# Attention scores issued further apart, and two splits moved behind the Gram masking, in a hybrid RWKV-7 and attention layer

## The chip, the cores and the metric

The kernel runs on one core of a Trainium2 chip. Its engines work at the same time, each through a list of its own in a fixed order: TensorE (PE in the profile; PEld are its weight loads), VectorE (DVE), ScalarE (ACT), GpSimd (POOL), and SyncE (SP), which here only issues DMAs. An instruction waits for semaphores that others raise, and everything behind it on its engine waits with it. The metric is the device time of one execution in microseconds; smaller is better.

## What is computed

One decoder layer for 256 tokens of width 1024, in float32. Two token mixers work on the same normalised input, and one combined projection `w_in` feeds both: RWKV-7 with eight heads of 64, a recurrence over time, and a softmax attention with eight heads, which for 256 tokens is one causal block. A gated feed-forward part with a short convolution follows. What bears on the change, cut from the reference:

```python
def step(state, inp):                       # RWKV-7, one token
    r_t, w_t, k_t, v_t, a_t, b_t = inp
    sa = jnp.einsum('bhvk,bhk->bhv', state, a_t)
    state = (state * w_t[:, :, None, :] + sa[..., None] * b_t[:, :, None, :]
             + v_t[..., None] * k_t[:, :, None, :])
    return state, jnp.einsum('bhvk,bhk->bhv', state, r_t)
...
bonus = (jnp.sum(rh * kh * r_k.astype(f32), axis=-1, keepdims=True) * vh).reshape(B, S, C)
g = jax.nn.sigmoid(xg) @ w_gate_up
return ((y + bonus) * g.astype(f32)).astype(z.dtype)
...
s_own = jnp.einsum('bhqd,bhkd->bhqk', q_c, k_own, preferred_element_type=f32) * scale
s_own = jnp.where(causal, s_own, -jnp.inf)
p = jax.nn.softmax(s_all, axis=-1).astype(v.dtype)
...
u_a = y_a @ w_branch_a[l]
u_b = y_b @ w_branch_b[l]
x = x + (g_a * u_a + g_b * u_b) @ w_out[l]
```

## The kernel before

**Matmuls in two halves.** A float32 operand is split in a high part (a cast to fp32r) and a low part (the rest), and three products are added: high by high, high by low, low by high. Every weight tile of 128x1024 goes through `load_next` (a DMA on SP into `raw`, four buffers), `split_hi` (L259, a cast on ACT, `whi`), `split_lo` (L269, a subtraction on DVE, `wlo`, three buffers), and is used by `wst` (L302, L304, L307) or `xst` (L323, L324, L327). Twelve of these matmuls are called a block here; two blocks use up a tile. A new load is issued when a split has freed its buffer, so weights run ahead of PE by a few tiles.

**Threads.** The projection, the recurrence and the attention are generators: `bulk`, `chain`, `att`, and `gn` for the group norm. Each yields two numbers, what it has just put on PE and how long it must now wait for others. A loop (from L1114) keeps a clock of its own and always resumes the first thread in its list that is due; so these numbers set the order in which instructions are written out. Behind that, the framework's scheduler orders each engine by its own estimate of times. On the chip the order is fixed.

**The recurrence in chunks of 64 tokens.** `chain` builds the decayed inputs AR and KB, then the Gram blocks: 64 matmuls in two groups (L668, `pgr`), each group of four PSUM banks multiplied by the mask `gmask` into G (L672, four operations of 128x512 a group). G's diagonal 16x16 blocks go out and back through DRAM by DMAs (L679, L681, into Tb), are inverted on DVE in fifteen dependent steps (L689, L691, ended by a copy, L692), and are scattered by 24 small DMAs into X (L694, L701; sixteen of the last on SP, eight on POOL). Meanwhile PE transposes v (L720, `pv`) and computes Z0 (L732, `pz`). From X the inverse of the 64x64 blocks is made by `below` (L750, `pp`), `masked` (P, L755), `plain` and `turned_` (L767 and L775, `px`) and additions to X (L760). Then come four chunks: L888 and L893, L896, L900, copies to VU (L903 on ACT, L904 on DVE), L910 (`pS`) and L922; the group norm of each chunk follows (L850 to L873) with a transposition on PE (L867, `pc`).

**Bonus and small up-projection.** `bp` is r times k times a column (L781, four operations on DVE, in place in zr). It is split into bph (L784, ACT) and bpl (L785, DVE). xg, the input of the small up-projection `w_gate_up`, is split into xgh (L787, ACT) and xgl (L788, with L791 twice for the short second part, DVE). PE uses them from L803 on. In the source these splits stand behind a wait of 11.5 units that follows Z0.

**Attention.** `att` starts when q, k and v are there. Scores are made in three groups, `parts`: the first 128 queries with all eight heads, then the last 128 with four heads twice. A group is written to two PSUM banks of the tag `at`, which has two in all (L993, `ps`). The diagonal part is masked on its way out by DVE (L996), and for the later queries the other half is copied out by ACT (L999). Then `softmax`: the maximum (L1004, L1005), an exponential for each head on ACT (L1008), the reciprocal (L1010) and the division (L1011). The loop is

```python
            for i, part in enumerate(parts):
                scores(*part)
                yield 0.9, 3.0
                softmax(*part)
```

After it the weights are transposed (L1021) and multiplied with v (L1033).

Of the kernel before, what the change touches and what calls it, by code (L numbers as in the profile page):

```python
# [9 lines left out]
F32 = mybir.dt.float32  # L10
F32R = mybir.dt.float32r
I32 = mybir.dt.int32
AF = mybir.ActivationFunctionType
OP = mybir.AluOpType
# [4 lines left out]
S = 256  # L19
# [18 lines left out]
def body(tc, x, positions, norm1_g, w_in, rwkv_mu, w_decay_up, decay_bias, w_aaa_up,  # L38
# [3 lines left out]
    act, dve, pool, pe = nc.scalar, nc.vector, nc.gpsimd, nc.tensor  # L42
    ctx = ExitStack()
    with ctx:
# [9 lines left out]
        def b8(name, shape):  # L54
            return sb.tile(shape, F32, name=name, tag="b8", bufs=5)

        def b4(name, shape=(128, 4, 256), dt=F32):
            return sb.tile(list(shape), dt, name=name, tag="b4", bufs=NB4)

        def by(name, shape=(128, 4, 256), dt=F32):  # L60

            return cst.tile(list(shape), dt, name=name, tag="by", bufs=4)

        def t1(name, shape=(128, 256), dt=F32):
            return sb.tile(list(shape), dt, name=name, tag="c1", bufs=8)

        def b2(name, shape, dt=F32):
            return sb.tile(shape, dt, name=name, tag="b2", bufs=9)
# [4 lines left out]
        def chp(name="ch"):  # L73
            return ps.tile([128, 512], F32, name=name, tag="ch", bufs=3)
# [41 lines left out]
        gmask = cst.tile([128, 128], F32, name="gmask")  # L116
# [35 lines left out]
        G1, MU, DB, AB, KK_, KA, RK, LG, LB, G2 = 0, 8, 23, 27, 31, 35, 39, 43, 47, 51  # L152
# [10 lines left out]
        def col(i):  # L163
            return par[:, i:i + 1]
# [337 lines left out]
        xg = b2("xg", [128, 2, S])  # L502
# [7 lines left out]
        def flat(t):  # L510
            return t.rearrange("p a b -> p (a b)")
# [7 lines left out]
        def bsl(q):  # L519

            return slice(64 * (1 - q), 64 * (1 - q) + 64)
# [12 lines left out]
        def gslot(ct, c=0):  # L534

            return 8 * (ct % 2) + 4 * (ct // 2) + c
# [13 lines left out]
        def chain():  # L550

            sg, av, kp = b4("sg"), b4("av"), b4("kp")
# [48 lines left out]
            for j in range(2):  # L601
                p = chp("prx").rearrange("p (a t c) -> p a t c", a=2, t=2)
                for a in range(2):
                    ct = 2 * j + a
                    for t in range(2):
                        pe.transpose(p[:, a, t], rx[:, t, ct * 128:ct * 128 + 128], ident)
                for a in range(2):
                    ct = 2 * j + a
                    dve.scalar_tensor_tensor(kk[:, ct], zk[:, ct], col(KK_ + ct),
                                             p[:, a].rearrange("p t c -> p (t c)"),  # L610
                                             op0=OP.mult, op1=OP.mult)
# [9 lines left out]
            def kb(q, u):  # L621
                return KB[half(q), 128 * u + 64 * q:128 * u + 64 * q + 128]
# [13 lines left out]
            zr = zs["r"]  # L636
# [5 lines left out]
            G = [b8(f"G{q}", [128, 16, 128]) for q in range(2)]  # L642
# [3 lines left out]
            def banks(nm):  # L646
                return [[(chp if j else atp)(nm) for _ in range(2)] for j in range(2)]
# [14 lines left out]
            for g in range(2):  # L662
                pg = [[p.rearrange("p (u i) -> p u i", u=4) for p in pj] for pj in banks("pgr")]
                for ct in (2 * g, 2 * g + 1):
                    for c in range(4):
                        u = 4 * ct + c
                        for q, hs in PAR:
                            pe.matmul(pg[ct % 2][q][:, c], kb(q, u), AR[hs, u].rearrange("p a i -> p (a i)"),  # L668
                                      start=True, stop=True)
                for ct in (2 * g, 2 * g + 1):  # L670
                    for q in range(2):
                        dve.tensor_tensor(G[q][:, gslot(ct):gslot(ct) + 4], pg[ct % 2][q],  # L672
                                          gmask[:, None, :].to_broadcast([128, 4, 128]), op=OP.mult)
                yield 2.1, (5.0, 0.1)[g]
            for q, hs in PAR:
                for b in range(4):
                    q0 = bsl(q).start + 16 * b
                    r0 = (q * 4 + b) * 16
                    nc.sync.dma_start(d1[r0:r0 + 16].rearrange("u (j i) -> j u i", j=16),  # L679
                                      G[q][q0:q0 + 16, :, 16 * b:16 * b + 16])  # L680
                nc.sync.dma_start(Tb[hs], d1[hs].rearrange("u (j i) -> u j i", j=16))  # L681
# [46 lines left out]
            for c in range(4):  # L728
                for j in range(2):
                    for q, a in QA:  # L730
                        ct = 2 * j + a
# [43 lines left out]
                        pe.matmul(p[bsl(a), i], P[bsl(a), i], X[bsl(a), 1, 8 * q + i], start=True, stop=True)  # L775
                return p

            yield 0, 11.5
            bp = zr
            for ct in range(4):  # L780
                dve.scalar_tensor_tensor(bp[:, ct], zr[:, ct], col(RK + ct), kp[:, ct],  # L781
                                         op0=OP.mult, op1=OP.mult)
            bph, bpl = by("bph", dt=F32R), by("bpl", dt=F32R)
            act.copy(flat(bph), flat(bp))  # L784
            dve.tensor_tensor(flat(bpl), flat(bp), flat(bph).bitcast(F32), op=OP.subtract)  # L785
            xgh, xgl = b2("xgh", [128, 2, S], F32R), t1("xgl", dt=F32R)
            act.copy(xgh, xg)  # L787
            dve.tensor_tensor(xgl, xg[:, 0], xgh[:, 0].bitcast(F32), op=OP.subtract)  # L788
            for r in (32, 96):
                ws = slice(r, r + 32)  # L790
                dve.tensor_tensor(xgh[ws, 1], xg[ws, 1], xgh[ws, 1].bitcast(F32), op=OP.subtract)  # L791
            yield 0, 2.0
            assert taken[0] == GATE_AT, taken[0]
            wgh, wgl = weights()
# [3 lines left out]
            for j in range(2):  # L798
                p, pg = chp(), chp("pg")
                for i in range(2):  # L800
                    ct = 2 * j + i
# [10 lines left out]
                for i in range(2):  # L812
                    ct = 2 * j + i
# [3 lines left out]
                                             op0=OP.add, op1=OP.mult)  # L817
# [61 lines left out]
            for c in range(4):  # L879
# [4 lines left out]
                if St is not None:  # L884
                    for j in range(2):
                        for q, a in QA:
                            ct = 2 * j + a
                            pe.matmul(pz[q][bsl(a), j], AR[half(q), 4 * ct + c, 0], St[half(q), ct],  # L888
                                      start=j == 0, stop=False, skip_group_check=True)
                    for j in range(2):  # L890
                        for q, a in QA:
                            ct = 2 * j + a
# [13 lines left out]
                if c < 3:  # L906
                    pS = chp("pS").rearrange("p (a n) -> p a n", a=8)
                    for h in range(8):
                        ct, q = divmod(h, 2)
# [9 lines left out]
                for j in range(2):  # L919
                    for q, a in QA:  # L920
                        ct = 2 * j + a
# [43 lines left out]
        def attention():  # L965
            qkT = []
            for i in range(2):
                dT = b4(f"qkT{i}")
                for j in range(2):
                    p = atp("pqk").rearrange("p (a t c) -> p a t c", a=2, t=2)  # L970
                    for a in range(2):
                        for t in range(2):
                            ct = 2 * j + a
# [12 lines left out]
            def scores(t, j, nh, sc):  # L986
                nk = 128 * (t + 1)
                ts = slice(t * 128, t * 128 + 128)
                pq = [atp("ps").rearrange("p (h k) -> p h k", k=nk) for q in range(2)]
                for i in range(nh // 2):  # L990

                    for q, hs in PAR:
                        pe.matmul(pq[q][:, i], qT[hs, 2 * j + i, ts], kT[hs, 2 * j + i, 0:nk],  # L993
                                  start=True, stop=True)
                for q in range(2):
                    dve.tensor_tensor(sc[:, q:nh:2, nk - 128:nk], pq[q][:, :, nk - 128:nk],  # L996
                                      cmask[:, None, :].to_broadcast([128, nh // 2, 128]), op=OP.add)
                    if t:
                        act.copy(sc[:, q:nh:2, 0:128], pq[q][:, :, 0:128])  # L999
# [40 lines left out]

            for i, part in enumerate(parts):
                scores(*part)
                yield 0.9, 3.0
                softmax(*part)
            yield 0, 4.0
            ybh = by("ybh", dt=F32R)
# [177 lines left out]
        for j in range(11):  # L1224
# [13 lines left out]
            for m in range(2):  # L1238
# [6 lines left out]
                                         op0=OP.mult, op1=OP.add)  # L1245
                dve.scalar_tensor_tensor(cv[:, 2:S], pm[:, 0:S - 2], cpar[:, n:n + 1], cv[:, 2:S],
                                         op0=OP.mult, op1=OP.add)
# [11 lines left out]
            if len(prev) == 2:  # L1259
# [3 lines left out]
        ws = [weights(), weights()]  # L1263
# [4 lines left out]
                                 op0=OP.mult, op1=OP.add)  # L1268
        for f, is_ in ((0, (0,)), (1, (0,)), (0, (1,)), (2, (0,)), (1, (1,)), (2, (1,)), (3, (0, 1)), (4, (0, 1))):
# [11 lines left out]
            if 1 in is_:  # L1281
                o = b2("o", [128, n])
                dve.scalar_tensor_tensor(o, fs, rs[:, t:t + 1], pre if f == 4 else x_sb[t][:, cs],
                                         op0=OP.mult, op1=OP.add)
# [25 lines left out]
```

## Time and profile before

| | us |
|---|---|
| median of three runs | 414.85 (414.8 to 416.55) |
| profiled execution | 414.23 |
| its span, first to last instruction | 412.5 |
| PE busy in the span | 402.8 |
| DVE busy | 325.8 |
| ACT busy | 232.8 |

The span is what the trace covers; the 1.73 us beside it belong to the start and the end of the execution. A row of the timeline gives start, duration, engine, line, operation, what is written from what, the count, and in brackets how long the engine stood idle ahead of it and what ended that. PEclk, in tenths, is the clock that TensorE was granted.

### The profile page before, as it was taken

How to read it: one execution, taken by the hardware profiler on the slowest of the kernel's cores; microseconds unless marked ns; L12 is line 12 of the kernel's file. 1: busy time of each engine (PE TensorE's matmuls, PEld its weight loads, DVE VectorE, ACT ScalarE, POOL GpSimd, SP SyncE). 2: the span in 40 equal slices, each digit the busy share in tenths (PEclk: the TensorE clock that was granted, in tenths of full speed). 3: DMA queues.
4: the chain of work that ended last, by engine and by line, in shares of the span. 5: the costliest groups of instructions: out<-in, count | busy, mean ns of one | idle time of the engine just before them, and what ended most of it. 6: DMA issues, size and time to landing. Idle time of an engine off the chain costs nothing.

```text
span 412.5 us, 8129 instructions
## 1 busy us (share of the span) xinstructions
PE 402.8 (98%) x3199; PEld 355.3 (86%) x3199; DVE 325.8 (79%) x564; ACT 232.8 (56%) x387; POOL 37.4 (9%) x61
## 2 busy tenths in 40 slices
PE   6999999999998999999999999999999999999996
PEld 3999989788997999999988887888888888888885
DVE  3888998969678867778974898979779678797784
ACT  6799655464454865453653884646446455464450
POOL 8900070000500010020000000000000000000000
PEclk9999999999998999999999999999999999999999
DMA  8945555562773332566564555765665666656612
GB/s 252 307 152 155 154 157 153 149 178 75 178 221 97 101 100 81 184 209 201 174 201 140 162 196 170 237 203 169 202 193 163 204 200 200 200 166 199 199 54 102
DMA packets 61991, 70.53 MB, mean 171 GB/s; under 512 B 9422, under 2 KB 52244, under 8 KB 61953
## 3 DMA queue, kind: packets, MB, share of 16 engines
q1 hardware_dynamic: 61104, 69.54, 56.0%
q0 software_dynamic: 832, 0.47, 0.6%
q8 instruction: 25, 0.41, 0.4%
q14 instruction: 14, 0.11, 0.1%
q10 hardware_dynamic: 16, 0.00, 0.0%
HBM read 68.56 MB, written 1.44 MB: 170 GB/s over the span
## 4 chain that ended last, share of the span: by engine, by line
PE 63%; DVE 8%; DMA 4%; ACT 2%; issue 2%; SPq 0%; DVEq 0%; ACTq 0%
PE acc L1198 12%; PE acc L1201 6%; PE acc L302 5%; PE acc L304 4%; PE f L1220 4%; PE acc L307 4%; PE f L1218 4%; PE f L1216 4%; PE at L1198 4%; DMA raw<-in_w_in_dram 3%; DVE wlo L269 2%; PE acc L323 2%; PE acc L327 2%; PE acc L324 2%; PE at L1201 2%
## 5 line engine op out<-in xcount | busy, mean ns | idle before, releaser
L259 ACT CAST whi<-raw 128x1024 fp32r<-128x1024 f32 x121 | 126.8, 1052 | 116.1 <-PE acc L1198 26.2
L269 DVE TENSOR_TENSOR wlo<-raw,whi 128x1024 fp32r<-128x1024 f32 x121 | 146.9, 1219 | 34.5 <-PE acc L1201 12.9
L1198 PE MATMUL acc<-hx,whi 128*128 128x512 f32 x264 | 72.3, 395 | 0.0
L302 PE MATMUL acc<-hx,whi 128*128 128x256 f32 x232 | 59.4, 291 | 0.0
L304 PE MATMUL acc<-hx,whi 128*128 128x256 f32 x232 | 56.9, 281 | 0.0
L1198 PEld LDWEIGHTS acc<-hx,whi 128*128 128x128 f32 x264 | 45.3, 188 | 6.3
L302 PEld LDWEIGHTS acc<-hx,whi 128*128 128x128 f32 x232 | 44.4, 191 | 1.8 <-issue 0.9
L1201 PEld LDWEIGHTS acc<-hx,wlo 128*128 128x128 f32 x264 | 40.2, 188 | 6.0
L304 PEld LDWEIGHTS acc<-hx,whi 128*128 128x128 f32 x232 | 44.4, 191 | 0.1
L1201 PE MATMUL acc<-hx,wlo 128*128 128x256 f32 x264 | 41.3, 278 | 0.0
L307 PE MATMUL acc<-hx,wlo 128*128 128x256 f32 x232 | 36.7, 281 | 0.0
L1220 PE MATMUL f<-wlo,hb 128*128 128x512 f32 x80 | 31.3, 391 | 0.4 <-DVE wlo L269 0.4
L307 PEld LDWEIGHTS acc<-hx,wlo 128*128 128x128 f32 x232 | 31.3, 191 | 0.3 <-issue 0.3
L1218 PE MATMUL f<-whi,hb 128*128 128x512 f32 x80 | 31.2, 390 | 0.0
L1216 PE MATMUL f<-whi,hb 128*128 128x512 f32 x80 | 31.2, 390 | 0.0
L1198 PE MATMUL at<-hx,whi 128*128 128x512 f32 x88 | 24.0, 394 | 0.0
L1206 DVE TENSOR_REDUCE an<-acc 128x256 f32<-128x512 f32 x22 | 15.0, 690 | 6.9 <-PE acc L1201 6.1
L323 PE MATMUL acc<-whi,hx 128*128 128x512 f32 x48 | 19.1, 398 | 0.0
L324 PE MATMUL acc<-whi,hx 128*128 128x512 f32 x48 | 18.8, 391 | 0.0
L1220 PEld LDWEIGHTS f<-wlo,hb 128*128 128x128 f32 x80 | 15.0, 188 | 3.9 <-DVE wlo L269 0.8
L1216 PEld LDWEIGHTS f<-whi,hb 128*128 128x128 f32 x80 | 15.0, 188 | 2.8
L1218 PEld LDWEIGHTS f<-whi,hb 128*128 128x128 f32 x80 | 15.0, 188 | 2.8
(321 smaller groups left out, 701.2 us busy)
## 6 DMA issues: line engine op xcount, KB each, us to landing
raw<-in_w_ffn_up_dram SPq DMA_DIRECT2D x44, 512.0 KB, 4.4
raw<-in_w_in_dram SPq DMA_DIRECT2D x37, 512.0 KB, 4.5
raw<-in_w_ffn_down_dram SPq DMA_DIRECT2D x22, 512.0 KB, 4.1
raw<-in_w_out_dram SPq DMA_DIRECT2D x8, 512.0 KB, 4.4
x<-in_x_dram SPq DMA_DIRECT2D x8, 256.0 KB, 4.7
early<-in_w_in_dram SPq DMA_DIRECT2D x4, 512.0 KB, 7.7
raw<-in_w_branch_b_dram SPq DMA_DIRECT2D x4, 512.0 KB, 3.5
raw<-in_w_branch_a_dram SPq DMA_DIRECT2D x4, 512.0 KB, 5.1
```

The costliest lines, as they stand in the source:

```text
L259: act.copy(wide(hi, k, c), spread(raw, k, c))
L269: eng.tensor_tensor(wide(lo, k, c), spread(raw, k, c), wide(hi, k, c).bitcast(F32), op=OP.subtract)
L302: pe.matmul(om, wh[:, k, ms], xh[:, k0 + k], start=k0 + k + m == 0, stop=False, skip_group_check=True)
L304: pe.matmul(om, wh[:, k, ms], xl[:, k0 + k], start=False, stop=False, skip_group_check=True)
L307: pe.matmul(om, wl[:, k, ms], xh[:, k0 + k], start=False, stop=k0 + k == nk - 1 and m == n - 1, skip_group_check=True)
L323: pe.matmul(ps_[t], xh[:, K, ts], wh[:, k], start=K == 0, stop=False)
L324: pe.matmul(ps_[t], xl[:, K, ts], wh[:, k], start=False, stop=False)
L1198: pe.matmul(ps_[m], wh[:, k, ms], hx[:, k0 + k].rearrange("p a s -> p (a s)"), start=k0 + k == 0, stop=False, skip_group_check=True)
L1201: pe.matmul(ps_[m][:, 0:S], wl[:, k, ms], hh[:, k0 + k], start=False, stop=k0 + k == 7, skip_group_check=True)
L1216: pe.matmul(fin[f], hb[:, 0, i, ts], wh[:, 0, cs], start=st, stop=False, skip_group_check=f == 3)
L1218: pe.matmul(fin[f], hb[:, 1, i, ts], wh[:, 0, cs], start=False, stop=False, skip_group_check=f == 3)
L1220: pe.matmul(fin[f], hb[:, 0, i, ts], wl[:, 0, cs], start=False, stop=False, skip_group_check=f == 3)
```

## The change

It is two edits. The second number of the yield behind each group of scores becomes 5.0 in the place of 3.0. And the fourteen lines that make bp, bph, bpl, xgh and xgl move from behind Z0 to behind the Gram blocks, inside `tc.issue_after(last_g)`: their instructions on DVE must stand behind the last masking operation of G on that engine. The wait of 11.5 where they stood becomes 11.0.

```diff
                 for ct in (2 * g, 2 * g + 1):
                     for q in range(2):
-                        dve.tensor_tensor(G[q][:, gslot(ct):gslot(ct) + 4], pg[ct % 2][q],
-                                          gmask[:, None, :].to_broadcast([128, 4, 128]), op=OP.mult)
+                        last_g = dve.tensor_tensor(G[q][:, gslot(ct):gslot(ct) + 4], pg[ct % 2][q],
+                                                   gmask[:, None, :].to_broadcast([128, 4, 128]), op=OP.mult).ins
                 yield 2.1, (5.0, 0.1)[g]
+            bp = zr
+            bph, bpl = by("bph", dt=F32R), by("bpl", dt=F32R)
+            xgh, xgl = b2("xgh", [128, 2, S], F32R), t1("xgl", dt=F32R)
+            with tc.issue_after(last_g):
+                for ct in range(4):
+                    dve.scalar_tensor_tensor(bp[:, ct], zr[:, ct], col(RK + ct), kp[:, ct],
+                                             op0=OP.mult, op1=OP.mult)
+                act.copy(flat(bph), flat(bp))
+                dve.tensor_tensor(flat(bpl), flat(bp), flat(bph).bitcast(F32), op=OP.subtract)
+                act.copy(xgh, xg)
+                dve.tensor_tensor(xgl, xg[:, 0], xgh[:, 0].bitcast(F32), op=OP.subtract)
+                for r in (32, 96):
+                    ws = slice(r, r + 32)
+                    dve.tensor_tensor(xgh[ws, 1], xg[ws, 1], xgh[ws, 1].bitcast(F32), op=OP.subtract)
...
-            yield 0, 11.5
-            bp = zr
...
+            yield 0, 11.0
             yield 0, 2.0
...
                 scores(*part)
-                yield 0.9, 3.0
+                yield 0.9, 5.0
                 softmax(*part)
```

The number of instructions of each kind stays the same; their order changes. Line numbers of the new kernel are 14 higher from the Gram blocks on and 1 higher behind the old place of the splits.

On DVE around the Gram masking, before (G_781 and G_782 are the two halves of G, by the parity of the head):

```order
L781 SCALAR_TENSOR_TENSOR zr<-zr,par,kp 128x256 x2
L486 SCALAR_TENSOR_TENSOR zv<-acc,par,zv 128x255
L269 TENSOR_TENSOR wlo<-raw,whi 128x1024
L781 SCALAR_TENSOR_TENSOR zr<-zr,par,kp 128x256
L785 TENSOR_TENSOR bpl<-zr,bph 128x1024
L672 TENSOR_TENSOR G_781<-pgr,gmask 128x512
L672 TENSOR_TENSOR G_782<-pgr,gmask 128x512
L672 TENSOR_TENSOR G_781<-pgr,gmask 128x512
L672 TENSOR_TENSOR G_782<-pgr,gmask 128x512
L269 TENSOR_TENSOR wlo<-raw,whi 128x1024
```

And after, from the second group of masks on (the first follows directly on a shift and a weight split):

```order
L672 TENSOR_TENSOR G_781<-pgr,gmask 128x512
L672 TENSOR_TENSOR G_782<-pgr,gmask 128x512
L672 TENSOR_TENSOR G_781<-pgr,gmask 128x512
L672 TENSOR_TENSOR G_782<-pgr,gmask 128x512
L680 SCALAR_TENSOR_TENSOR zr<-zr,par,kp 128x256 x4
L685 TENSOR_TENSOR xgl<-xg,xgh 128x256
L688 TENSOR_TENSOR xgh<-xg,xgh 32x256 x2
L269 TENSOR_TENSOR wlo<-raw,whi 128x1024
L683 TENSOR_TENSOR bpl<-zr,bph 128x1024
L269 TENSOR_TENSOR wlo<-raw,whi 128x1024
```

The bonus product and bpl stood ahead of the first masks and now stand behind the last; xgl and xgh, which stood farther down among the steps of the inversion, have come up to the same place.

On PE around the scores, before (a row of L307 stands for a whole block of the projection; the numbers tell tiles apart):

```order
L775 MATMUL px<-X,P 64x64 x16
...
L307 MATMUL acc<-hx,wlo 128x256 x4
L993 MATMUL ps<-qkT_1572,qkT_1505 128x256 x4
...
L307 MATMUL acc<-hx,wlo 128x256 x4
...
L775 MATMUL px<-X,P 64x64 x16
L993 MATMUL ps<-qkT_1572,qkT_1505 128x256 x4
...
L775 MATMUL px<-X,P 64x64 x32
```

And after, from the same px on (L789 is the old L775, L994 the old L993):

```order
L789 MATMUL px<-X,P 64x64 x16
L994 MATMUL ps<-qkT_1572,qkT_1505 128x256 x4
...
L307 MATMUL acc<-hx,wlo 128x256 x4
...
L789 MATMUL px<-X,P 64x64 x32
...
L307 MATMUL acc<-hx,wlo 128x256 x4
L994 MATMUL ps<-qkT_1572,qkT_1505 128x256 x4
...
L307 MATMUL acc<-hx,wlo 128x256 x4
L901 MATMUL pb<-Z_1241,X 64x64 x8
```

The second group of scores stands where the third stood, and the third follows two blocks, the 32 matmuls of px and one more block later.

On DVE around the copies to VU, before:

```order
L1005 TENSOR_SCALAR mx<-mx 128x4
L269 TENSOR_TENSOR wlo<-raw,whi 128x1024
L1010 RECIPROCAL sm<-sm 128x4
L904 COPY VU<-pb 64x2x64
L1011 TENSOR_TENSOR sc_1645<-sc_1645,sm 128x1024
L904 COPY VU<-pb 64x2x64
```

And after (L997 is the old L996, L1005 the old L1004, L905 the old L904, L1011 and L1012 the old L1010 and L1011):

```order
L1011 RECIPROCAL sm<-sm 128x4
L1012 TENSOR_TENSOR sc_1645<-sc_1645,sm 128x1024
L269 TENSOR_TENSOR wlo<-raw,whi 128x1024
L997 TENSOR_TENSOR sc_1645<-ps,cmask 128x2x128 x2
L1005 TENSOR_REDUCE mx<-sc_1645 128x4
L905 COPY VU<-pb 64x2x64 x2
```

The copies stood behind the third group's maximum already; now its masks, a weight split and the division of the second group stand right ahead of them too.

More of the change, by code (lines that the diff above doesn't have):

```diff
@@ L776, in turned_ @@
                 return p
-            yield 0, 11.5
-            bp = zr
[L780 to L791, printed above, removed]
+            yield 0, 11.0
             yield 0, 2.0
```

## The prediction

> **What bounds the kernel now.** I read the page first. PE, TensorE's matmuls, is busy for nearly the whole span, and one slice of its clock row stands below 9.
>
> ```profile
> span 412.5 us, 8129 instructions
> PE 402.8 (98%) x3199; PEld 355.3 (86%) x3199; DVE 325.8 (79%) x564; ACT 232.8 (56%) x387; POOL 37.4 (9%) x61
> PEclk9999999999998999999999999999999999999999
> ```
>
> So time can come only from the few places where PE stands still or runs slowly. The list of PE's waits has six rows. Three belong to the first steps (L413, L109, L456); these are the others, the last of them from the feed-forward stage.
>
> ```profile
> PE ps L993 <- ACT sc L999: 1.7, 1, 1.7
> PE pv L720 <- DVE G L672: 0.6, 1, 0.6
> PE f L1220 <- DVE wlo L269: 0.4, 1, 0.4
> ```
>
> The view by windows gives both places their price. Columns: busy time and count of PE, PEld, DVE, ACT, POOL, then the granted clock and the DMA.
>
> ```profile
> 79.40:82.20 2.80, 2.19 (x65) 1.98 (x64) 2.80 (x5) 1.86 (x3) 0.00 (x0) 1.00 0.78 217
> 127.40:130.80 3.40, 1.66 (x26) 1.31 (x20) 1.90 (x5) 2.45 (x13) 0.00 (x0) 1.00 0.56 158
> 130.80:134.20 3.40, 3.40 (x16) 3.14 (x15) 3.40 (x8) 0.28 (x1) 0.00 (x0) 0.50 0.00 1
> 134.20:137.60 3.40, 3.40 (x77) 3.21 (x76) 2.63 (x4) 3.40 (x12) 0.00 (x0) 1.00 0.19 22
> ```
>
> At 79.4 PE loses 2.80 - 2.19 = 0.61 us. At 127.4 it loses 1.74 us, and in the next 3.40 us the granted clock is 0.50: full PE, half the work. The slow stretch has no other cause in sight than the idle time just before it, so the scores cost twice. The timelines of PE and ACT show how:
>
> ```profile
> 123.13 1.13 PE L993 MATMUL ps<-qkT,qkT 64*128 64x256 f32 x8
> 125.81 1.16 PE L750 MATMUL pp<-X,G 64*64 64x64 f32 x64
> 126.79 1.10 PE L775 MATMUL px<-X,P 64*64 64x64 f32 x32
> 129.63 1.50 PE L993 MATMUL ps<-qkT,qkT 64*128 64x256 f32 x8 [1.74 <-ACT sc L999]
> 135.47 2.08 PE L775 MATMUL px<-X,P 64*64 64x64 f32 x64
> 140.42 0.46 PE L900 MATMUL pb<-Z,X 64*64 64x64 f32 x16
> ```
> ```profile
> 119.47 1.04 ACT L259 CAST whi<-raw 128x1024 fp32r<-128x1024 f32 x1 [1.06 <-DMA raw<-in_w_in_dram]
> 126.14 0.40 ACT L1008 ACTIVATE sc<-sc,mx 128x128 f32<-128x128 f32 x1 [1.27 <-DVE mx L1005]
> 129.23 0.61 ACT L999 COPY sc<-ps 128x256 f32<-128x256 f32 x2
> 133.92 0.51 ACT L1008 ACTIVATE sc<-sc,mx 128x256 f32<-128x256 f32 x1 [4.07 <-DVE mx L1005]
> 135.90 0.62 ACT L999 COPY sc<-ps 128x256 f32<-128x256 f32 x2
> 142.38 0.43 ACT L903 COPY VU<-pb 64x128 f32<-64x128 f32 x2
> ```
>
> The second group of scores is done at 124.3, but its copies out of PSUM (L999) stand on ACT behind the eight exponentials of the first group (126.14 to 129.2). The third group needs those banks and comes too soon.
>
> **The change part by part.** Lines are those of before.
>
> *Scores further apart.* On PE the second group moves behind one more block of the projection and behind pp and px, that is to where the third stood; the third moves behind two blocks, px (64) and one block more. A block is half of what lies between 137.55 and 140.42, about 1.45 us. With everything 0.6 earlier, PE goes: px until 121.0, two blocks to 123.9, pp 124.9, px 125.9, second scores 127.0, two blocks 129.9, px (64) 131.9, block 133.4, third scores 134.5, block 135.9, L900 136.4, two blocks 139.3, then pS (L910). What are the others' times? DVE's rows:
>
> ```profile
> 104.98 0.39 DVE L692 COPY Xb<-Xb 128x256 f32<-128x256 f32 x1
> 120.55 1.23 DVE L269 TENSOR_TENSOR wlo<-raw,whi 128x1024 fp32r<-128x1024 f32 x1 [1.88 <-ACT whi L259]
> 121.69 1.28 DVE L996 TENSOR_TENSOR sc<-ps,cmask 128x512 f32<-128x512 f32 x2
> 123.01 1.22 DVE L1004 TENSOR_REDUCE mx<-sc 128x8 f32<-128x1024 f32 x1
> 124.14 1.87 DVE L760 TENSOR_TENSOR X<-X,px 128x512 f32<-128x512 f32 x3
> 129.59 1.23 DVE L1011 TENSOR_TENSOR sc<-sc,sm 128x1024 f32<-128x1024 f32 x1
> 133.73 0.75 DVE L996 TENSOR_TENSOR sc<-ps,cmask 128x256 f32<-128x256 f32 x2
> 142.68 0.28 DVE L904 COPY VU<-pb 64x128 f32<-64x128 f32 x1
> ```
>
> The softmax is late at its root: DVE stands 1.88 us at 120.55 for a weight cast, the cast for a DMA, and that DMA for SP's queue:
>
> ```profile
> 104.97 1.39 SPq L694 DMA_DIRECT2D d<-Xb  x2
> 107.74 7.59 SPq L701 DMA_DIRECT2D X<-d  x16
> 115.42 36.74 SPq L236 DMA_DIRECT2D raw<-in_w_in_dram  x10
> ```
>
> The weights are issued (115.42) behind the sixteen scatters of X, and these follow the end of the inversion on DVE (104.98). Whether that comes earlier decides the margins (next part; I take 2 us). Then the cast goes at 117.7, when ACT is free of its copies, the split ends at 119.9, masks 121.1, maximum 122.3, the three additions to X 124.1: pp, which waits for the second of them (123.5), finds it done at 123.9. Exponentials 124.3 to 127.4. In the new order DVE then has a split, P, one X addition, L1011 to 128.8, masks of the second group to 129.5; ACT copies one half, casts a weight (1.04), copies the other, to 130.8. The third scores come at 133.4: margin 2.6 us where 1.74 was missing. The wait goes, and with it the half clock.
>
> What is late next? The copies of VU (L903, L904) that pS needs now stand behind the third group's masks, L999 and maximum. Second maximum 132.0, four exponentials to 134.2 (2.0, as 133.92 to 135.90), L1011 135.7, a split 136.8, masks 137.5, copies 137.8, maximum 139.0, VU 139.5. PE is there at 139.3: a new wait of 0.2. The next, for the first transposed output (L867), comes out 0.3 us short in the same way, since one more L1011 (1.2) and a split stand ahead of yc. I take 0.5 for both together; ends 0 and 2.5, the error of ten rows added up.
>
> *Splits behind the masking.* These are the moved steps and what they stood before:
>
> ```profile
> 70.38 0.48 DVE L781 SCALAR_TENSOR_TENSOR zr<-zr,par,kp 128x256 f32<-128x256 f32 x1
> 71.97 1.23 DVE L785 TENSOR_TENSOR bpl<-zr,bph 128x1024 fp32r<-128x1024 f32 x1 [1.11 <-ACT bph L784]
> 73.11 2.48 DVE L672 TENSOR_TENSOR G<-pgr,gmask 128x512 f32<-128x512 f32 x4
> 79.19 2.48 DVE L672 TENSOR_TENSOR G<-pgr,gmask 128x512 f32<-128x512 f32 x4
> 85.32 1.23 DVE L269 TENSOR_TENSOR wlo<-raw,whi 128x1024 fp32r<-128x1024 f32 x1 [2.52 <-issue]
> 89.96 0.41 DVE L788 TENSOR_TENSOR xgl<-xg,xgh 128x256 fp32r<-128x256 f32 x1
> 100.68 0.42 DVE L791 TENSOR_TENSOR xgh<-xg,xgh 32x256 fp32r<-32x256 f32 x1
> ```
>
> From 70.38 to 73.11 the first four masks stand behind 2.7 us of bonus work and its wait for ACT; that is gone, and two splits and two shifts behind them move up too. The second four can then follow the last Gram matmul (77.8) directly: third mask done at about 78.7 and not 81.0, while pv's second bank is reached near 80.3. The 0.61 us go. What is moved (four products, 1.6; three small splits, 1.2; bpl, 1.2: 4.0 us) lands after the masks, where DVE idles 2.52 at 85.32. In front of it stands one weight split, held up some 0.6 us; wlo has three buffers, so the split runs up to two tiles of 2.9 us ahead of PE, and nothing waits: 0 (0.6 if that lead were used up). ACT's two casts move with it into its own idle time.
>
> The inversion gains the 0.41 + 0.41 + 0.42 us that stood in its way at 90 and 100, plus some of the 2.3 us by which G is finished earlier, of which SP's second load of Tb, behind a weight load that waits for PE, keeps back about 1.5. Bounds are 1.2, if nothing of that comes through, and 3.5, if all does; 1.24 + 0.8 = 2.0 us is the value used above.
>
> *Sum.* Profiled time 414.23 (the span 412.5 and 1.73 around it). pv: -0.61. Scores: -1.74. Half clock: 3.40 x 0.5 = -1.70. New waits: +0.5. Together -3.55, so 410.7 for the profiled execution; the median of the three runs, 414.85, stands 0.62 above that one, and 414.85 - 3.55 gives 411.3. Behind 142 us PE has no wait longer than 0.4, so what is won at 130 stays won.
>
> [...]
>
> **The rivals.**
>
> *VU too late (the slower end).* If the second group's exponentials end L us later than 134.2, pS waits L + 0.2, since five DVE steps and the copies (5.3 us) lie between. From about 1.7 us of idle time on, the half clock comes back as well (+1.70). Slower than before it becomes when L + 1.70 exceeds 3.55, so from L = 1.9 on, and by over 0.5% from 3.9 on; at L = 4.8 the time is 411.3 + 4.8 + 1.7 = 417.8. For it: the copies now stand behind a whole softmax step; before, they were only 0.3 us behind the last exponential. Against: PE waits for ACT's second copy with a margin of 2.6, and nothing on ACT waits for more than weights that landed long ago. Chance 0.13, of which 0.06 beyond 0.5%.
>
> *The inversion isn't earlier.* Then the additions to X end at 125.3 (second of three from 124.14) and pp waits 1.4 us at 123.9: 411.3 + 1.4 = 412.7. Should this bring the half clock, 414.4. For it: SP's queue is strict, and the Tb load has a weight load ahead. Against: 1.24 us of the gain are removed instructions. Chance 0.15.
>
> *The half clock stays.* Some 3.40 us at 0.50 turn up although PE waits nowhere over 1 us, and 1.70 of the gain is lost: 413.0. [...] Chance 0.10.
>
> That the change doesn't move the scores is no rival; the order of instructions shows the move.
>
> **How the numbers follow.** Forecast 0.62, rivals 0.13, 0.15, 0.10. No new wait at all gives 410.8, and pv's wait is 0.8 if counted by the pitch of its matmuls: lower end 410.2. The upper end takes in the pp wait with its half clock, 414.4. A measurement of this kernel tells about 0.5%, or 2.1 us, from no change: below 412.8 is faster. Faster: 0.58 of the forecast, 0.09 of the inversion's case and 0.05 of VU's, 0.72. Slower: 0.06. Same: 0.22.
>
> **What would show it.** Right: no wait of ps for L999, no slice below 9 in the clock row between 5 and 412, third G mask before pv's second bank, first weight load after the X scatters 2 us earlier against PE. Wrong: a wait of PE over 1.7 us at pp, pS (L910) or pc (L867), followed by a window at 0.50, or the half clock without a wait.

## The result, and the profile after

The changed kernel takes 411.87 us (median of eight runs, 410.6 to 412.77) against 414.83 for the kernel before in runs beside it (413.65 to 416.55): a ratio of 0.9921, 95% interval 0.9896 to 0.9945, so 2.3 to 4.3 us less. The forecast was 411.3 (410.2 to 414.4). Two later comparisons gave 0.9922 and 0.9934. The number held; one of the four terms behind it did not, and another was too small. By the shift of the line numbers the old L750 is L764 here, L993 is L994 and L867 is L868.

From the page of the changed kernel's profiled execution (412.34 us): the span, the busy times, the clock row.

```profile
span 410.6 us, 8130 instructions
PE 401.7 (98%) x3199; PEld 353.5 (86%) x3199; DVE 325.0 (79%) x564; ACT 232.8 (57%) x387; POOL 36.2 (9%) x61
PEclk9999999999999999999999999999999999999999
```

The slice below 9 is gone. So are PE's waits at ps and pv; behind the first steps its list of waits reads now:

```profile
PE px L789 <- issue: 1.3, 1, 1.3
PE f L1221 <- DVE wlo L269: 0.5, 1, 0.5
PE pc L868 <- ACT pT L1023: 0.5, 1, 0.5
```

The view by windows at the same two places, columns as before:

```profile
79.80:82.60 2.80, 2.80 (x69) 2.60 (x69) 2.77 (x8) 2.31 (x4) 0.00 (x0) 1.00 0.23 26
127.40:130.80 3.40, 3.40 (x33) 2.96 (x30) 3.37 (x7) 1.04 (x6) 0.00 (x0) 1.00 0.42 142
130.80:134.20 3.40, 3.40 (x77) 3.21 (x76) 3.17 (x5) 2.35 (x6) 0.00 (x0) 1.00 0.36 63
```

PE is busy throughout at a clock of 1.00. In this profile SP's queue shows an earlier inversion: the copies of the inverted blocks go out at 103.32 (104.97 before), and the weight loads behind the scatters at 113.80 (115.42 before).

```profile
103.32 1.39 SPq L708 DMA_DIRECT2D d<-Xb  x2
...
106.11 7.58 SPq L715 DMA_DIRECT2D X<-d  x16
113.80 2.20 SPq L236 DMA_DIRECT2D raw<-in_w_in_dram  x4
```

And the timeline of PE has something new, in the middle of px:

```profile
120.03 0.86 PE L789 MATMUL px<-X,P 64*64 64x64 f32 x23
122.16 0.45 PE L789 MATMUL px<-X,P 64*64 64x64 f32 x9 [1.27 <-issue]
...
127.49 1.14 PE L994 MATMUL ps<-qkT,qkT 64*128 64x256 f32 x8
...
135.07 1.13 PE L994 MATMUL ps<-qkT,qkT 64*128 64x256 f32 x8
```

The second and third scores follow without a wait. But between the 23rd and the 24th of 32 equal matmuls PE stops for 1.27 us, and the profile shows nothing that it waits for. The page lists a queue of kind instruction, q8, with 25 packets and 0.41 MB, so 16 KB each, and PE has 3199 matmuls and 3199 weight loads. If these packets carry PE's code, a piece holds about 256 of these instructions by that count (an estimate). The times agree: the 25 pieces start from 20.65 to 393.19 us, and PE runs 6042 matmuls and weight loads in between, 252 for each of the 24 steps (153 to 448 in single ones, 237 to 265 in the last seven). One piece runs from 119.63 to 120.76, and PE goes on 1.40 us after its end. The view of the DMA while this piece runs:

```profile
q1 hardware_dynamic: 451, 0.45, 104.0%
q8 instruction: 1, 0.02, 5.4%
```

By that view the sixteen DMA engines are full (q1 104.0%, q8 5.4%), nearly all of it with q1, on which the weight loads run. So part of the gain was given back at px, and the question is where the rest came from: by its own terms the forecast had only 0.5 us for new waits.

### The profile page after: what moved, and what is told of

The parts are those of the page before. It is cut to its first block, busy times and chain, and to the rows that moved or that the text cites. A ratio compares the mean times of both kernels' runs of the same rounds, so it can differ in the third digit from the quotient of the medians.

```text
span 410.6 us, 8130 instructions
## 1 busy us (share of the span) xinstructions
PE 401.7 (98%) x3199; PEld 353.5 (86%) x3199; DVE 325.0 (79%) x564; ACT 232.8 (57%) x387; POOL 36.2 (9%) x61
## 4 chain that ended last, share of the span: by engine, by line
PE 88%; DVE 4%; ACT 3%; DMA 2%; issue 1%; SPq 0%; ACTq 0%
PE acc L1199 12%; PE acc L302 9%; PE acc L304 8%; PE acc L307 8%; PE acc L1202 6%; PE acc L323 5%; PE acc L327 4%; PE acc L324 4%; PE f L1221 4%; PE f L1219 4%; PE f L1217 4%; PE at L1199 4%; PE at L1202 2%; DVE wlo L269 2%; DMA x<-in_x_dram 1%
## 5 line engine op out<-in xcount | busy, mean ns | idle before, releaser
L302 PE MATMUL acc<-hx,whi 128*128 128x256 f32 x232 | 58.5, 288 | 0.0
L304 PE MATMUL acc<-hx,whi 128*128 128x256 f32 x232 | 56.1, 278 | 0.0
L1199 PEld LDWEIGHTS acc<-hx,whi 128*128 128x128 f32 x264 | 45.3, 188 | 6.3
L302 PEld LDWEIGHTS acc<-hx,whi 128*128 128x128 f32 x232 | 43.6, 188 | 1.8 <-issue 0.8
L304 PEld LDWEIGHTS acc<-hx,whi 128*128 128x128 f32 x232 | 43.7, 188 | 0.1
L307 PE MATMUL acc<-hx,wlo 128*128 128x256 f32 x232 | 36.0, 278 | 0.0
L307 PEld LDWEIGHTS acc<-hx,wlo 128*128 128x128 f32 x232 | 30.8, 188 | 0.3 <-issue 0.3
```

Source lines behind the costliest of these rows:

```text
L302: pe.matmul(om, wh[:, k, ms], xh[:, k0 + k], start=k0 + k + m == 0, stop=False, skip_group_check=True)
L304: pe.matmul(om, wh[:, k, ms], xl[:, k0 + k], start=False, stop=False, skip_group_check=True)
L307: pe.matmul(om, wl[:, k, ms], xh[:, k0 + k], start=False, stop=k0 + k == nk - 1 and m == n - 1, skip_group_check=True)
L1199: pe.matmul(ps_[m], wh[:, k, ms], hx[:, k0 + k].rearrange("p a s -> p (a s)"), start=k0 + k == 0, stop=False, skip_group_check=True)
```

## The experiments

Each group of comparisons ran on one chip; the kernel before took 415.58 (first four kernels), 415.04 (next four) and 414.74 us (last three).

### The spacing alone

The kernel before with this line only:

```diff
-                yield 0.9, 3.0
+                yield 0.9, 5.0
```

> Only the wider spacing of the scores, the splits at their old place; TensorE's order is that of the changed kernel, VectorE's differs. Theory A (the wait of the scores for the copies on ScalarE and the half clock that it sets off are the gain, the moved splits give the wait at pv and the earlier inversion): no wait at ps, no window at 0.50 between 5 and 410 us, the 0.6 to 0.8 us wait at pv stays, and pp waits about 1.4 us for the additions to X, because the inversion and so the weights behind it come no earlier. Gain 3.4 - 1.4 - 0.3 = 1.7 us: 413.1. Theory B (the half clock has nothing to do with the wait): a window at 0.50 is still there, gain 1.7 - 1.7 = 0: 414.8. Theory C (the splits alone make the gain): 414.8, with a wait left in the scores.

413.96 us, ratio 0.9954 (0.9934 to 0.9974). PE's instructions stand as in the changed kernel. Its waits, without those of the first steps and f's:

```profile
PE pc L867 <- DVE yc L860: 0.7, 1, 0.7
PE pv L720 <- DVE G L672: 0.6, 1, 0.6
...
PE pp L750 <- DVE X L760: 0.4, 2, 0.3
...
PE pS L910 <- DVE VU L904: 0.2, 1, 0.2
```

The wait of ps and the half clock are gone, and pv is left as it was. But in place of 1.7 + 1.7 us the gain is 1.6, and three waits stand in the list that the first profile of before does not have.

### The splits alone

The changed kernel with the spacing of before:

```diff
-                yield 0.9, 5.0
+                yield 0.9, 3.0
```

> Only the moved splits, the spacing of the scores as before; TensorE's order is that of the kernel before. Theory A: pv's wait goes (0.8 us), the softmax comes about 1.9 us earlier and TensorE 0.8 us earlier, so the third group's wait for ScalarE's copies shrinks from 1.7 to about 0.6 us, too short to bring the half clock: gain 0.8 + 1.1 + 1.7 = 3.6 us, 411.2, as much as both edits together. Theory B: wait 0.6 us and the half clock all the same: gain 1.9 us, 412.9. Theory C (the spacing alone makes the gain): 414.0, with the full wait of 1.7 us.

413.32 us, ratio 0.9939 (0.9917 to 0.9961). The two longest waits behind the first steps:

```profile
PE pb L901 <- DVE X L774: 1.2, 2, 0.9
PE px L789 <- issue: 0.7, 1, 0.7
```

The list has no wait at ps, but only since PE stopped at px, 0.7 us, or 0.88 by the pitch (counted from start to start of neighbouring matmuls, against the same rows without a stop): the third scores start at 128.16, and the copies of the second group end at 128.29. Without that stop PE would have waited some 0.9 us, so the splits alone take about half of the wait away. New is a wait at pb, the first matmul of the chunks (L900 of before), for the last additions to X. It was in no list so far, and neither the kernel with the spacing alone nor the changed kernel has it: where the spacing is wider, it is gone.

### PE kept busy in the wait

The kernel before; one `turned_` runs its sixteen matmuls (32 in the trace) three times, so that PE has 1.87 us more to do ahead of the third scores: px takes 2.97 us there for 96 matmuls and 1.10 for 32 before. The order on DVE and ACT changes a little, too:

```diff
-            def turned_(q, P):
+            def turned_(q, P, times=1):
...
-                for i in range(8):
+                for i in list(range(8)) * times:
...
-            pt = turned_(1, P[1])
+            pt = turned_(1, P[1], 3)
```

> The kernel before, with the 16 paired matmuls of px (32 in all) that stand ahead of the third scores written three times in the place of once, into the same bank with the same result: about 1.9 us more work for TensorE at the place where it waits 1.74 us. Nothing else moves on TensorE. Theory A (idle time sets off the half clock): the wait shrinks to about 0, no window at 0.50, gain 1.7 us or a little less: 413.1, although TensorE does more. Theory B (the half clock is not due to the idle time): the window at 0.50 stays, time as before or up to 0.2 us more: 414.8 to 415.0.

416.81 us, ratio 1.0030 (1.0010 to 1.0051): no gain, but a loss of 0.1 to 0.5%. The view by windows, and the row of PE at pb:

```profile
127.40:130.80 3.40, 3.40 (x120) 3.31 (x114) 1.90 (x5) 2.92 (x15) 0.00 (x0) 1.00 0.57 147
139.40:142.80 3.40, 1.54 (x24) 1.22 (x23) 2.35 (x5) 2.25 (x9) 0.00 (x0) 1.00 0.58 154
142.80:146.20 3.40, 3.40 (x19) 3.40 (x18) 3.37 (x6) 3.33 (x7) 0.00 (x0) 0.50 0.00 0
```
```profile
141.10 0.33 PE L900 MATMUL pb<-Z,X 64*64 64x64 f32 x2 [1.59 <-DVE X L760]
```

The wait at ps is filled, and the slow window behind it is gone. Both turn up again 12 us later, at pb. In this one execution the half clock went where the idle time went, which speaks for the stall as its cause; the counts over many runs, further down, say more. It also says that something other than ps holds PE at pb.

### PE's code moved by 46 instructions

The changed kernel; the second of two `keep_warm(2)` in the first 9 us, where PE only bridges the time until the input arrives, becomes 25 small matmuls:

```diff
-                    keep_warm(2)
+                    for _ in range(25):
+                        pe.matmul(idle[0:64, 0:16], ones[:, 0:64], ones[:, 0:16], start=True, stop=True)
```

> The changed kernel with 46 more instructions at the start of TensorE's program (25 tiny matmuls with their weight loads in the place of 2 warming ones, in a gap where TensorE waits for the normalised input), so that everything behind stands 46 instructions later in the code. Theory A (the 1.3 us at px that wait for nothing shown are a late load of code, 16 KB or 256 instructions at a time): the stop at px goes, or moves by 46 instructions; with it gone 1.3 us less than the changed kernel's profile, about 410.6. Theory B (px waits for data, the scattered X): the stop stays at the same matmul of px, 411.9.

411.76 us, ratio 0.9906 (0.9879 to 0.9932).

```profile
121.03 1.15 PE L790 MATMUL px<-X,P 64*64 64x64 f32 x32 [0.89 <-issue]
```

The stop moved from the 24th matmul to the first: 23 matmuls with their weight loads, exactly the 46 instructions. So it hangs on the place in the program, not on the data. The author reads it as PE running to the end of the code it had; no view shows that directly.

### The kernel before, twice more

> The kernel before, unchanged, for a second profile. In the runs timed so far beside the experiments, 8 of 22 executions of it show a mean granted clock of 0.994 to 0.996, 14 show 0.998 to 1.0; the first profile was one of 0.996. [...] Theory B (the half clock belongs to every execution): a window at 0.50 right behind the wait again.

> The kernel before once more, for a third profile: as e5. [...] Theory B: half clock in all three.

414.09 and 415.60 us. These two are the key to the rest. PE's waits in the second profile of before, and its rows at both places:

```profile
PE ps L993 <- ACT sc L999: 1.3, 1, 1.3
...
PE pb L900 <- DVE X L760: 0.9, 2, 0.6
PE pv L720 <- DVE G L672: 0.6, 1, 0.6
```
```profile
129.64 1.39 PE L993 MATMUL ps<-qkT,qkT 64*128 64x256 f32 x8 [1.34 <-ACT sc L999]
133.90 2.08 PE L775 MATMUL px<-X,P 64*64 64x64 f32 x64
139.55 0.33 PE L900 MATMUL pb<-Z,X 64*64 64x64 f32 x2 [0.63 <-DVE X L760]
140.15 0.46 PE L900 MATMUL pb<-Z,X 64*64 64x64 f32 x14 [0.27 <-DVE X L760]
```

Neither execution has a half clock (both clock rows are all 9), and both wait at pb, as the first did not: 0.9 us, in the third profile too, or 1.27 by the pitch of the matmuls. DVE's row for the additions on which pb waits, in the first profile of before, with the half clock, and then in the second, without:

```profile
138.82 1.28 DVE L760 TENSOR_TENSOR X<-X,px 128x512 f32<-128x512 f32 x2
```
```profile
138.82 1.28 DVE L760 TENSOR_TENSOR X<-X,px 128x512 f32<-128x512 f32 x2
```

The same time to a hundredth. In the third profile both the first masks and these additions come 1.57 us later (123.27 and 140.39): 17.1 us lie between them in all three. So in this stretch DVE and ACT are the path; whether PE runs at half clock from 130.8 to 134.2 doesn't reach it. PE comes to L900 at 140.42 slow. Fast, it would come at about 138.8 (four matmuls of L307 from 138.30 on), but it waits until 139.55 and again until 140.15. The block behind pb starts at these times, first slow, then fast:

```profile
140.81 0.38 PE L302 MATMUL acc<-hx,whi 128*128 128x256 f32 x1
```
```profile
140.53 0.38 PE L302 MATMUL acc<-hx,whi 128*128 128x256 f32 x1
```

That is 0.28 us for the slow window, in this pair of executions. The timed runs agree: in 59 runs of before beside these experiments, 23 have a mean granted clock of 0.994 to 0.996, as the first profile (0.996; a window of 3.41 us at a half costs 0.004), and their median is 415.39; 36 have 0.998 to 1.0, and theirs is 415.10. A slow window is there in four of ten executions (where in the span, the timed runs don't tell), and by these medians it costs 0.3 us. The size is rough: in the three groups taken apart the medians differ by 1.3, 0.1 and 0.6 us. The third experiment is the contrast: in its profile the slow window stands behind pb, where no listed wait follows until the feed-forward stage that could hide it. Its seven runs with a slow window have a median of 417.58, its five without one 416.05: there it costs 1.5 us.

### The changed kernel again, and its code further off

> The changed kernel, unchanged, for its time on the same chip and a second profile. Theory A (PE's code comes late at px in every execution, since the weights now load earlier): a wait without a releaser of 0.7 to 1.4 us at px (L789) again, 0.4 to 0.7 us at the first pc (L868), no half clock between 5 and 409 us, and 0.8% less than the kernel before. Theory B (the late code was chance of one execution): no wait above 0.3 us at px; then the gain of most executions is about 4 us, 1.0%.

411.53 us, ratio 0.9922 (0.9898 to 0.9946). In this profile px doesn't stop, but pp waits, and pS, beside pc:

```profile
PE pc L868 <- DVE yc L861: 0.6, 1, 0.6
...
PE pp L764 <- DVE X L774: 0.5, 2, 0.3
PE pS L911 <- DVE VU L905: 0.2, 1, 0.2
```

So the stop at px, 1.3 us in the first profile, is no fixed cost. The wait at pp has its root on DVE, in front of the masks of the first scores:

```profile
120.03 1.22 DVE L269 TENSOR_TENSOR wlo<-raw,whi 128x1024 fp32r<-128x1024 f32 x1 [2.21 <-ACT whi L259]
121.18 1.28 DVE L997 TENSOR_TENSOR sc<-ps,cmask 128x512 f32<-128x512 f32 x2
```

A weight split that waits 2.21 us for a cast, and the cast for its DMA, keeps the masks and the additions to X behind it. To move the code out of this stretch altogether, a hundred more small matmuls went into the first 9 us (58 and four wide ones for eight wide, 25 for two, twice):

> The changed kernel with 100 more small matmuls on PE in the first 9 us, where it only keeps busy until the input arrives (fewer wide ones beside them), so 200 more instructions ahead of everything: the block of PE's code that came late at px then begins 100 matmuls earlier, in a stretch in which PE runs a projection block and pp, and is asked for before the four weight loads of 113.8 us. Theory A (the code's DMA stands behind those loads, 3.1 to 4.0 us long, and PE runs into the end of its code): the code lands within 1.5 us of being asked for, px (L789) has no wait above 0.2 us, and the time is 1.0 to 1.4 us below the changed kernel's. Theory B (something else holds PE at px, such as the copies of P): the wait stays at the same matmul of px, and the time is the same within 0.4 us. Either could be hidden if another block of code then comes late elsewhere; that shows as a wait without a releaser.

416.45 us, ratio 1.0038 (1.0022 to 1.0054). This decides nothing on the code: the profile shows no stop at px, but neither did the unchanged kernel's above, and the start spoils the time (last section).

### That split on POOL

The changed kernel; the 34th low half is made by POOL, and the rest of the order is as it was:

```diff
-                raw, hi, k, c = halves.pop(0)
+                (raw, hi, k, c), eng = halves.pop(0), pool if nlo[0] == 34 else eng
```

> The changed kernel with one weight split (wlo, L269) on POOL instead of DVE: the one that stands on DVE ahead of the masks of the first scores and waited 1.47 and 2.21 us for its cast in the two profiles of the changed kernel; POOL takes about 2.6 us for it, by its two halves of L436 (2.55). Nothing else moves in the order. Theory A (without the late code of px, PE waits at pp, 0.83 us by pitch, because DVE adds px to X late, and DVE is late because that split waits for a weight DMA): L997 starts 1.1 to 2 us earlier against the first scores, pp has no wait, and the time is 0.5 to 1.0 us below the changed kernel's where px isn't held up by code. Theory B (the waits at px and pp are both the late code or late P): pp's wait stays at 0.4 us or more. Slower by 1 us or more would be the low half coming late from POOL: then PE waits for wlo.

> The changed kernel for its time on the same chip as these two, and a third profile. Theory A (a late code load and a late X take each other's place in front of pp): either a wait at px without a releaser and none at pp, or one at pp for L774 and none at px, 0.8 to 1.5 us in all; pS and pc 0.7 to 1.3 us in all; no half clock between 10 and 405 us. Theory B (the first profile's late code was the rule, the second the exception): px waits 0.7 us or more.

411.06 us, ratio 0.9905 (0.9879 to 0.9931), beside 411.79, ratio 0.9934 (0.9911 to 0.9958), for the changed kernel. In the third profile of the changed kernel, a long execution (414.39 us), the split waits 3.13 us and pp 1.8:

```profile
PE pp L764 <- DVE X L774: 1.8, 2, 1.6
```
```profile
122.01 1.23 DVE L269 TENSOR_TENSOR wlo<-raw,whi 128x1024 fp32r<-128x1024 f32 x1 [3.13 <-ACT whi L259]
```

With the split on POOL, DVE's masks wait for nothing but the scores, and of PE's listed waits behind 16 us pc's alone is left beside f's:

```profile
118.67 1.29 DVE L997 TENSOR_TENSOR sc<-ps,cmask 128x512 f32<-128x512 f32 x2 [1.00 <-PE ps L994]
```
```profile
119.86 2.38 POOL L269 TENSOR_TENSOR wlo<-raw,whi 128x1024 fp32r<-128x1024 f32 x1 [7.02 <-ACT whi L259]
```
```profile
PE pc L868 <- ACT pT L1023: 0.3, 1, 0.3
```

A short stop of px, 0.32 us, is not in the list (the 32 matmuls take 1.42 us in the place of 1.10). The next version, with the same split on POOL, has no such stop and no wait at pp either. That shows pp's wait to be this split's doing. The time is 0.7 us below the changed kernel's by the medians, but the intervals overlap: a version at least as good, not shown to be better. It beats the kernel before by 0.7 to 1.2%.

A second split on POOL, the one ahead of the masks of the third scores (`nlo[0] in (34, 37)`), went too far:

> As e9, with a second split on POOL: the one that stands ahead of the masks of the third scores, 137.28 in the second profile of the changed kernel. DVE's copies of VU then come about 1.2 us earlier, and the scheduler also puts one split behind the chain to yc. Theory A (pS waits 0.39 and the first pc 0.84 us because DVE is full there): both waits fall below 0.2 us, and the time is 1 us below e9's. Theory B (pc waits for POOL's power, 1.04 us, and ACT): pc keeps 0.5 us or more, and the time is within 0.4 us of e9's.

413.14 us, ratio 0.9962 (0.9942 to 0.9983). With it the framework ordered DVE and ACT anew, and waits elsewhere outweigh what pc gained (its wait is gone):

```profile
PE pb L901 <- DVE Z L897: 1.2, 1, 1.2
...
PE pS L911 <- DVE VU L905: 0.4, 1, 0.4
```

## Why the prediction was right, and where it was not

The numbers of the table are waits as the list of waits gives them, behind the first 16 us and without f's, which every profile has. "Rest" is the span less the waits and less 1.7 for a slow window.

| profile | span | waits and slow window | rest |
|---|---|---|---|
| before, first | 412.5 | ps 1.7, half clock 1.7, pv 0.6 | 408.5 |
| before, second | 412.3 | ps 1.3, pb 0.9, pv 0.6 | 409.5 |
| before, third | 413.8 | ps 1.6, pb 0.9, pv 0.6, acc 0.5, px 0.4 | 409.8 |
| changed, first | 410.6 | px 1.3, pc 0.5 | 408.8 |
| changed, second | 410.9 | pc 0.6, pp 0.5, pS 0.2 | 409.6 |
| changed, third | 412.6 | pp 1.8, pc 0.7, pS 0.2 | 409.9 |
| changed, split on POOL | 409.4 | pc 0.3 | 409.1 |

**The accounting holds to 1.4 us**: without waits every version comes to 408.5 to 409.9. So most of what tells these executions apart is PE's waits, as the prediction said. The rest is not constant, partly because the list counts short: pb's 0.9 are 1.27 by the pitch, and the 0.32 us in px of the version on POOL are not in it.

**pv, -0.61: right.** The wait is gone in every profile with the moved splits and there in every one without.

**Scores, -1.74: right in size.** The wait at ps was 1.7, 1.3 and 1.6, and is gone; the margin came out at 3.2 us (copies of the second group done at 131.9, third scores at 135.07; 2.6 was forecast). The spacing alone is enough for that, the splits alone leave about half.

**Half clock, -1.70: this step failed.** The prediction took the slow window's cost from PE alone (full PE, half the work) and went on that "what is won at 130 stays won", since PE had no wait longer than 0.4 behind it. PE had none because it came late. The profile showed one execution of a kind that makes up four in ten, and there the slow clock stood in front of a wait of 0.9 us, 1.27 by the pitch, and hid it. The net price is 0.3 us by the timed runs and 0.28 by the pair of profiles; by terms 1.70 - 1.27 = 0.43. What the change removes in an execution without a slow window (two of the three profiles, six in ten timed runs) is the wait at pb, which the prediction did not know. That this wait is of the size of the term is luck, and it kept the sum near the measured time. The first two experiments show that it goes with the spacing. On DVE the last two additions to X stood behind the maximum of the third scores and a division (138.82 in the rows above); in the changed kernel they stand ahead of the third scores' masks:

```profile
133.27 1.28 DVE L774 TENSOR_TENSOR X<-X,px 128x512 f32<-128x512 f32 x2
...
138.06 0.75 DVE L997 TENSOR_TENSOR sc<-ps,cmask 128x256 f32<-128x256 f32 x2
```

**New waits, +0.5: too small in the three profiles.** pc took 0.5 to 0.7 in the place of 0.3, pS 0 to 0.2 as forecast. Not foreseen was the start of the stretch: 1.3 us at px, put down to late code, or 0.5 to 1.8 at pp from a late weight. The prediction let the splits and casts run at 117.7, when ACT is free; in the three profiles of the changed kernel this cast started at 117.79, 118.95 and 120.93, each time held by its DMA. The weight loads behind the scatters had been issued from 113.80, 114.99 and 115.48 on (115.42 in the first profile of before, and 2 us less was forecast). From there to the cast it took 4.0, 4.0 and 5.5 us, against 4.05 before. So in the second profile the issue was late, in the third the load as well. The rival "The inversion isn't earlier" had priced this wait at pp (1.4), and in part it came true: the copies of the inverted blocks went out at 103.32, 104.00 and 104.13, against 104.97, 104.59 and 106.18 in the three profiles of before, 1.4 us earlier by the means and not 2.0.

**The other rivals.** VU was not late: pS waited 0.2 us at most. The half clock did not stay: in 22 of 23 timed runs of the changed kernel the mean clock is 0.998 or more, and so it is in 51 of 52 runs of the other experiments, the third left out. In before it is so in 36 of 59, in the third experiment, with 1.9 us of waiting at pb, in 5 of 12. These counts tie the slow window to the long waits at ps and pb, though not every long wait brings one: 1.7 us at ps was followed by a half clock in the first profile of before, and 1.9 in two pieces at pb in the third experiment, but none followed 1.3 and 1.6 at ps in the second and third profile of before, nor 1.8 in two pieces at pp in the third of the changed kernel. So the 1.7 us from which on the prediction has the half clock come back is an estimate from one wait; no run shows a limit, nor what else decides. The chance of 0.10 for a half clock without a long wait was the author's estimate. Of the profiled executions only the first of before and the third experiment's have a mean clock below 0.998 (0.996 both), and both had a long wait.

**The range.** Its lower end, 410.2, does not follow from its terms: 410.8 without new waits, less 0.19 for pv by the pitch, is 410.6. Nothing hung on it, as the measured median lies above both.

**What stays open.** The means of the three profiled executions differ by 1.5 us (414.64 and 413.13), the timed medians by 3.0 to 3.5. The three of the changed kernel were all longer than the medians beside them (412.34, 412.67, 414.39 against 411.87, 411.53, 411.79), so they probably wait more than the usual execution; what the usual one waits, no profile here shows. So the gain of 3.0 to 3.5 us is measured, but its split into terms is shown for single executions only. Whether PE stops at px for late code, and that because of the earlier loads or by chance, was not settled either: the stop at px was 0.4 in one of three profiles of before, and 1.3 in one of three of the changed kernel.

## What to carry to other kernels

A slow clock on one engine may cost less than it takes there: here 1.70 us on PE came to 0.28 in front of a wait for DVE, and to 1.5 where no such wait followed. So look at when the others' work behind it is done (here DVE's X at 138.82 in both executions), not at how full the slow engine is. A profile is one execution; where a stretch holds a matter of chance (a slow clock, a stop without a releaser, a weight that comes late), take two or three profiles and the clocks of the timed runs before putting a price on it. And an operation that waits for a DMA was badly placed in front of a chain on DVE: the split stood there 2.21 and 3.13 us for its cast, and pp waited 0.5 and 1.8; on an idle POOL, at 2.38 us in the place of 1.22, pp had no wait.

## What the runs showed of the hardware

- The half clock came in some executions of a kernel and not in others. Waits of PE of 1.7 us in one piece (first profile of before) and 1.9 in two (third experiment) were followed by one stretch at 0.50, of 3.41 us in the first profile of before and over a window of 3.40 in the third experiment; others of 1.3 and 1.6 (second and third profile of before) and 1.8 (in two pieces, third of the changed kernel) were not. By the mean clock it was in 23 of 59 runs of before and in 7 of 12 of the third experiment.
- In the first profile of the changed kernel 25 packets of 16 KB on the queue of kind instruction start between 20.65 and 393.19 us, about 256 matmuls and weight loads for each by the count above (an estimate). With 64 matmuls of px started in 1.0 us ahead of it and q1, with loads of 512 KB, at 104.0%, PE stopped there for 1.3 us inside the next px, named "issue" in the list of waits; other profiles list 0.4, 0.7 and 0.9 at px. With 46 more instructions ahead the stop came 23 matmuls and their weight loads earlier, which suggests the end of a piece. In other profiles of before and of the changed kernel the list has none.
- In the first 16 us the granted clock of the view by windows did not tell how fast PE was. With 108 small matmuls (16 columns) in the place of wide ones, eight transpositions of xt took 1.97 us each time, against 1.11 and 1.09 in the changed kernel's first profile at the same places, though the windows say 1.00 for both. The first projections were slow until about 16 us (sixteen matmuls in 3.10 us, 2.38 in the changed kernel's first profile), and the next stage started at 19.90 and not at 16.94, 3 us later. With 25 small ones only, in the fourth experiment, the transpositions took 1.18 and 1.09.

```profile
8.09 1.97 PE L416 MATMUL xt<-ident,xn 128*128 128x128 f32 x8
...
11.42 1.97 PE L416 MATMUL xt<-ident,xn 128*128 128x128 f32 x8
13.04 3.10 PE L460 MATMUL acc<-hx,whi 128*128 128x256 f32 x16
```

- A split of 128x1024 took 2.38 us on POOL (the version with one split there) and 1.22 on DVE (the changed kernel's second profile).
